# Moving one weight tile by 192 bytes and reordering two attention value products behind gate products

## The chip, the cores and the metric

The kernel runs on one core of one Trainium2 chip. The metric is the device time of one launch in microseconds (us), as the median of several runs. The layer has a batch of one, 512 positions and a model width of 1024, all in float32.

## What is computed

One decoder block with two mixers side by side, followed by a gated feed-forward. The core of the reference, shortened:

```python
h = rmsnorm(x, norm1_g)
a_b, a_c, a_x, q, kc, vc, ksl, vsl, kwn, vwn, g_nsa, g_merge = split(h @ w_in)
y_a = a_b * causal_dwconv(a_c * a_x, conv_a_w)
...                                    # q, k: norm and rotation; k_cmp, v_cmp: compressed keys and values
y_b = nsa(q, k_cmp, v_cmp, k_sel, vsl, k_win, vwn, sigmoid(g_nsa))
gm = sigmoid(g_merge)
x = x + (gm[:D] * (y_a @ w_a_out) + gm[D:] * (y_b @ w_b_out)) @ w_o
gu = rmsnorm(x, norm2_g) @ w_ffn_in
g = causal_dwconv(gu[:F], ffn_conv_w) + ffn_conv_b
x = x + (silu(g) * gu[F:]) @ w_ffn_out          # F = 2816
```

`nsa` has three branches per head: compressed keys, selected blocks and a sliding window. With 512 positions the selected blocks are all blocks, so the second and third branch are both plain causal attention with different keys and values.

## The kernel before

**Split products.** Every float32 operand is cut into a high and a low part in a faster format (`F32R` in the code). A product `w @ x` is then three products on PE: `wh@xh`, `wh@xl`, `wl@xh`. The helper `dense` issues first all `wh@xh` and `wh@xl` of an output tile (lines L437 and L438 of the profile), then all `wl@xh` (L440). The list that it returns holds only the first kind, in order: for a gate tile with eight input tiles these are 16 products, numbered 0 to 15.

**Order of work.** The program text lists the work stage by stage, but the order on each engine is made when the program is built. A planner goes through the instructions with its own estimates of their durations and starts on each engine the ready instruction that was written earliest. Each engine then runs its list strictly in order. `behind(later, earlier)` adds one rule for the planner: on that engine, `later` comes after `earlier`. It adds no wait to the running program.

**Attention.** `attend(pt_, g, qt)` handles one of two key groups `g` (four heads) for one block `qt` of 128 queries. Blocks are taken in the order 3, 2, 1, 0, and for each block `g` is 0 and then 1. For each branch `br` (1 first, then 0) PE makes the scores of each head into one of three banks of tag `s` (L665 and L666; L691 for block 0), DVE adds the mask and takes the maximum (L717, L718), ACT takes the exponential and thereby empties the bank (L719) and scales it (L725). The weights are then turned: a transpose on DVE (L652), four DMAs to memory and one back into a tile `tn` (`turn`). For each key tile `kt` ACT copies the high part (`ph`, L749), POOL subtracts it in place (L750), and PE adds two products to the block's accumulator `po`: the high product `ph` (L752) and the rest product (L759). They add to one accumulator and are issued in the order high, rest, high, rest. In branch 0 two products with the compressed values stand behind the first high product (L757); they need the tile `pc` that ACT writes at L743. At the end ACT copies half of the accumulator (`yt`, L761).

**Gate tiles.** `gate_tile(j, t)` makes one of 16 tiles of the merge gates. Its 24 products go to a bank of tag `d`. There are two such banks, and the conv tiles `pa`, the gate tiles `pg` and the mixer-A products `pma` take them in turn. In program order the stretch in question reads `pg2, pg3, pma2, pma3, pg4`, so `pg4` takes the bank that `pma2` had. That bank is emptied by DVE at L824. The planner fills PE with these products while attention waits for other engines. Two rules are written already: the first high product of block (g=0, qt=3) comes after product 6 of gate tile 0, and that of (g=0, qt=0) after product 10 of gate tile 13.

**Feed-forward.** Pairs of feed-forward tiles are computed as a Strassen product: seven products of half size instead of eight. `xf_h` and `xf_l` hold seven sums of input tiles as moving operands of 256 columns. `ff_forms` makes the weights' forms. `a22` is one quarter of the weights that is used as it is; its high part is the tile `th` (written by ACT at L173) and its low part the tile `tl`. The other forms are in `sh`, `sl` and in the ring `wh_s`, `wl_s`. The tiles lie one after another in each partition in the order of their first use; `gap_...` tiles hold nothing and only shift what follows. In the part that matters here the sizes in bytes of a partition are:

```
xf_h   4*7*256*4 = 28672
xf_l   4*7*256*4 = 28672
th     2 buffers of 2048
gap_w  48*4 = 192
tl     2 buffers of 2048
...    sf, sh, sl, p1: all multiples of 1024
```

Of the kernel before, what the change touches and what calls it, by code (L numbers as in the profile page):

```python
# [11 lines left out]
F32 = mybir.dt.float32  # L12
# [6 lines left out]
P = 128  # L19
# [66 lines left out]
def tile_block(ctx: ExitStack, tc: tile.TileContext, xT, pos, par, par2, w_tok, w_a3, w_gate, w_ao, w_bo, w_o,  # L86
               w_ff, w_dn, c_w1, out):
    nc = tc.nc
# [11 lines left out]
    def const(shape, name, dt=F32, pool=sb):  # L100
        return pool.tile(shape, dt, name=name, tag=name)
# [17 lines left out]
    def s_bank(name):  # L119
        return bank("s", name, 3)  # L120
# [3 lines left out]
    def t_bank(name, i=None):  # L124
        if i is None:
            i = len(n_t) % 2
            n_t.append(name)
        return bank(f"t{i}", name, 1)
# [55 lines left out]
    def ring_w(src, name):  # L184
        raw = raw_tile(name)
        nc.sync.dma_start(raw, src)
        h, l = ring(name)
        split(h, l, raw)
        return h, l
# [39 lines left out]
    def behind(later, earlier):  # L229

        tc.add_manual_dep(later.ins, earlier.ins.name,
                          mybir.DependencyInfo(mybir.DependencyClass.NoSync, mybir.DependencyReason.DATA),
                          reason="order")
# [206 lines left out]
            nc.tensor.matmul(acc, wl, xh, start=False, stop=last and i == len(units) - 1)  # L440
        return ops

    gate_ops, value_op = {}, {}

    def w_units(w, xh, xl, nk, k0=0, koff=0):
        wh, wl = w
# [6 lines left out]
    kHH, kL = kk[:, 0], kk[:, 1]  # L453
# [176 lines left out]
    def by_head(v, b):  # L630

        return v.rearrange("p (q a b i) -> p a b q i", q=QB, a=2, b=2)[:, :, b]

    def attend(pt_, g, qt):
        nk = (qt + 1) * P
        off = NC if qt < NT - 1 else 0
        q = qT[qt]
# [3 lines left out]
        def small(name, n, dt=F32):  # L641
            pool = pxg if name in ("mx1", "mx0", "sums1") else pb if name in ("sums0", "mcs") else pt_
            return pool.tile([P, HG, n], dt, name=f"{name}{tag}", tag=name, bufs=2)

        def e_tile(br, n):
            return pt_.tile([P, HG * S], F32, name=f"e{tag}{br}", tag="e", bufs=NE)[:, 0:n * HG * P].rearrange(
                "p (b k h i) -> p b k h i", b=QB, k=n, h=HG)

        def turn(e, n, e_name):

            v = e.rearrange("p b k h i -> p (b k h i)")
            nc.vector.transpose(v, v)  # L652
            w = n * P
            dst = pt_.tile([P, HG * S], F32R, name=f"tn_{e.name}", tag="tn", bufs=NTN)[:, 0:QB * w]
            d = dst.bitcast(F32)
            mid = dr.tile([QB, QB, SQ, w], F32, name=f"td_{e.name}", tag=f"td_{e.name}", bufs=1)
            for a in range(QB):
                nc.sync.dma_start(mid[a].rearrange("b j r -> j b r"),
                                  v[a * SQ:(a + 1) * SQ].rearrange("p (b r) -> p b r", b=QB))
            turned_dma[e_name] = nc.sync.dma_start(d.rearrange("p (a r) -> p a r", a=QB), mid.rearrange("a b j r -> (b j) a r"))  # L660
            return dst.rearrange("p (a k r) -> p a k r", a=QB, k=n)

        def scores(w, i, br, a, b):
            h = g * HG + i
            nc.tensor.matmul(w, q[:, h, :], kHH[:, 2 * br + g, a:b], start=True, stop=False)  # L665
            nc.tensor.matmul(w, q[:, h, :], kL[:, 2 * br + g, a:b], start=False, stop=True)  # L666

        def scale_of(sums, br):
            nc.vector.reciprocal(sums, sums)
            nc.gpsimd.tensor_mul(sums, sums, gates[:, :, br:br + 1])  # L670
# [10 lines left out]
        acc4 = acc.rearrange("p (a r) -> p a r", a=QB)  # L681
        if qt == 0:
# [4 lines left out]
            for i in range(HG):  # L687
                sc = s_bank(f"sc{tag}{i}")
                w = sc[:, 0:2 * (NC + P)].rearrange("p (b k) -> p b k", b=2)
# [15 lines left out]
        for br in (1, 0):  # L705
            if qt > 0:
                o = off if br == 0 else 0
                e = e_tile(br, qt + 1)
                mx = small(f"mx{br}", 1)
                sums = small(f"sums{br}", 1)  # L710
                for i in range(HG):
                    sc = s_bank(f"sc{tag}{i}{br}")
                    scores(sc[:, 0:o + nk], i, br, NC - o, NC + nk)
                    if o:
                        nc.vector.tensor_add(xc[:, i, :], sc[:, 0:NC], cm_add[:, qt, :])
                    dg = sc[:, o + nk - P:o + nk]
                    nc.vector.tensor_add(dg, dg, causal)  # L717
                    nc.vector.tensor_reduce(mx[:, i], sc[:, o:o + nk], axis=AX.X, op=ALU.max, negate=True)  # L718
                    nc.scalar.activation(e[:, :, :, i].rearrange("p b k i -> p k b i"),  # L719
                                         sc[:, o:o + nk].rearrange("p (k b i) -> p k b i", b=QB, i=SQ), AF.Exp,  # L720
                                         bias=mx[:, i], accum_out=sums[:, i])
                scale_of(sums, 1 + br)
                for i in range(HG):
                    v = e[:, :, :, i]
                    nc.scalar.activation(v, v, AF.Copy, scale=sums[:, i])  # L725
                turned = turn(e, qt + 1, (g, qt, br))
            if br == 0:
                mcs = small("mcs", 2)
                mc, sc_ = mcs[:, :, 0:1], mcs[:, :, 1:2]
                nc.vector.tensor_reduce(mc[:, :, 0], xc, axis=AX.X, op=ALU.max, negate=True)  # L730
                for i in range(HG):
                    nc.scalar.activation(xc[:, i], xc[:, i], AF.Exp, bias=mc[:, i], accum_out=sc_[:, i])
                scale_of(sc_, 0)
                nc.gpsimd.tensor_tensor(xc, xc, sc_.to_broadcast([P, HG, NC]), op=ALU.mult)
                xs = small("xs", 2 * NC, F32R)
                nc.scalar.activation(xs[:, :, 0:NC], xc, AF.Copy)
                nc.gpsimd.tensor_sub(xs[:, :, NC:], xc, xs[:, :, 0:NC].bitcast(F32))
                pt = t_bank(f"ptc{tag}", 0)
                for a in range(2):
                    nc.tensor.transpose(pt[:, a * P:(a + 1) * P],  # L740
                                        xs[:, 2 * a:2 * a + 2, :].rearrange("p h c -> p (h c)").bitcast(F32), ident)
                pc = pt_.tile([P, 2, P], F32R, name=f"pc{tag}", tag="pc", bufs=1)
                nc.scalar.activation(pc, pt[:, 0:2 * P].rearrange("p (a t) -> p a t", a=2), AF.Copy)  # L743
            k0 = br if qt == 0 else 0
            for kt in range(qt + 1):
                pl = turned[:, :, kt + k0]
                pt = pl.bitcast(F32)
                ph = pt_.tile([P, QB, P], F32R, name=f"ph{tag}{kt}{br}", tag="pth", bufs=NPT)
                nc.scalar.activation(ph, pt, AF.Copy)  # L749
                nc.gpsimd.tensor_sub(pl, pt, ph.bitcast(F32))  # L750
                w = v_t[:, kt, 2 * br + g, :]
                hi = nc.tensor.matmul(acc4, w, ph, start=kt == 0 and br == 1, stop=False)  # L752
                if kt == 0 and br == 1:
                    value_op[g, qt] = hi
                if kt == 0 and br == 0:
                    for b in range(2):
                        nc.tensor.matmul(by_head(acc, b), vc_t[:, b, g, :], pc.rearrange("p a (q i) -> p a q i", i=SQ),  # L757
                                         start=False, stop=False)
                nc.tensor.matmul(acc4, w, pl, start=False, stop=kt == qt and br == 0)  # L759
        tmp = pt_.tile([HD, 512], F32, name=f"yt{tag}", tag="yt", bufs=1)  # L760
        nc.scalar.activation(tmp, acc[HD:, :], AF.Copy)  # L761
        yo = pt_.tile([P, 2, P], F32, name=f"yo{tag}", tag="yo", bufs=1)
# [86 lines left out]
    for qt in QT_ORDER:  # L849
        for g in range(G):  # L850
            attend(pt_, g, qt)
# [18 lines left out]
    for i in range(4):  # L870
# [3 lines left out]
        w = ring_w(w_bo[i], f"bo{i}")  # L874
# [8 lines left out]
                                           op0=ALU.mult, op1=ALU.subtract)  # L883
    for w, step in (("ao1", (1, 3, 1)),):
        behind(raw_dma[w], turned_dma[step])
    for step, j, n in (((0, 3), 0, 6), ((0, 0), 13, 10),):
        behind(value_op[step], gate_ops[j][n])
    nc.scalar.activation(warm[:, 0:1], tb[KD - 1][:, 0:1], AF.Silu)
    in_ctx.close()

# [9 lines left out]
    xf_h = const([P, 4, 7, TH], "xf_h", F32R, px)  # L900
    xf_l = const([P, 4, 7, TH], "xf_l", F32R, px)
    pw = ctx.enter_context(tc.tile_pool(name="pw", bufs=1, side="left"))
    pw.tile([P, D // 2], F32R, name="th_", tag="th", bufs=2)
    const([P, 48], "gap_w", F32, pw)

    def x_forms(k, v):
        nc.vector.tensor_sub(v[:, T1:T3 + 1], v[:, 1:4:2], v[:, 0:2])
# [5 lines left out]
    for n, j in enumerate(O_ORDER):  # L913
        w = ring_w(w_o[j], f"o{j}")
# [275 lines left out]
```

## Time and profile before

| what | value |
|---|---|
| median of 3 runs | 696.2 us (695.93 to 697.58) |
| the profiled execution | 696.92 us, of which the span from the first to the last instruction is 695.1 us |
| PE busy | 689.2 us, 99% of the span, 4111 products |
| DVE, ACT, POOL busy | 74%, 63%, 36% of the span |
| granted TensorE clock | 1.000 |
| DMA | 124.87 MB, mean 180 GB/s |

The page gives the busy time of each engine. A busy PE may still be slower than it could be: what shows it is the distance from the start of one product to the start of the next. That distance is read from rows of the timeline, where the first column is the start in us and the second the duration. A mark in brackets at the end of a row is idle time of the engine just before it and what ended it.

### The profile page before, as it was taken

To read this page: it belongs to the slowest core of one execution; us is meant where nothing else is said; L and a number is where in the kernel's file an instruction comes from. 1 tells how busy PE (TensorE), PEld (TensorE's weight loads), DVE (VectorE), ACT (ScalarE), POOL (GpSimd) and SP (SyncE) were. 2 spreads that over 40 slices of the span, in tenths; PEclk is the share of its full clock that TensorE was granted. 3 is DMA by queue.
4 is the path that set the end of the run, shared out by engine and by line. 5 is a ranking of instruction groups with operands and counts; after the bars stand their busy time and mean duration, and the time that the engine had idled before them with its cause. 6 is when DMAs were issued, how large, how long until landed. Compare 5 with 4: busy or idle time off the path is not lost.

```text
span 695.1 us, 11268 instructions
## 1 busy us (share of the span) xinstructions
PE 689.2 (99%) x4111; PEld 614.5 (88%) x4111; DVE 511.7 (74%) x897; ACT 436.7 (63%) x776; POOL 248.7 (36%) x247
## 2 busy tenths in 40 slices
PE   9999999999999999999999999999999999999997
PEld 9999888887878888788889999999999999999986
DVE  6987886766566546475888999898787787877543
ACT  7635654878888866535776857665566655566530
POOL 4041443477788867462112212121122211112110
PEclk9999999999999999999999999999999999999999
DMA  8333686568666654563586977997877979775665
GB/s 268 113 98 122 170 194 145 132 240 237 222 222 228 195 169 124 193 229 118 130 198 160 219 192 167 245 218 180 215 173 180 210 172 227 174 175 112 132 137 152
DMA packets 57623, 124.87 MB, mean 180 GB/s; under 512 B 5344, under 2 KB 21088, under 8 KB 57568
## 3 DMA queue, kind: packets, MB, share of 16 engines
q1 hardware_dynamic: 35648, 79.39, 35.3%
q0 software_dynamic: 14848, 32.51, 27.4%
q10 hardware_dynamic: 7072, 12.26, 5.5%
q8 instruction: 32, 0.52, 0.3%
q14 instruction: 23, 0.19, 0.1%
HBM read 111.55 MB, written 12.58 MB: 179 GB/s over the span
## 4 chain that ended last, share of the span: by engine, by line
PE 95%; ACT 2%; DMA 1%; POOL 1%; DVE 1%; issue 0%; SPq 0%; ACTq 0%; POOLq 0%
PE p L438 10%; PE p L437 10%; PE p L440 10%; PE pdn L438 6%; PE pdn L437 6%; PE pdn L440 6%; PE pg L437 4%; PE pg L438 4%; PE pg L440 3%; PE pa L438 3%; PE pa L437 3%; PE pa L440 3%; PE po L438 2%; PE po L440 2%; PE po L437 2%; PE pj_s L269 2%
## 5 line engine op out<-in xcount | busy, mean ns | idle before, releaser
L437 PE MATMUL p<-xf_h,sh 128*128 128x256 f32 x336 | 80.6, 277 | 0.0
L438 PE MATMUL p<-xf_l,sh 128*128 128x256 f32 x336 | 80.5, 276 | 0.0
L175 POOL DMA_DIRECT2D wl_s<-in_w_ff_dram x22 | 19.6, 891 | 156.1 <-ACT wl_s L174 154.8
L438 PE MATMUL pdn<-al,wh_d 128*128 128x512 f32 (+1 forms) x176 | 68.5, 389 | 0.0
L437 PE MATMUL pdn<-ah,wh_d 128*128 128x512 f32 (+1 forms) x176 | 68.3, 389 | 0.0
L438 PEld LDWEIGHTS p<-xf_l,sh 128*128 128x128 f32 x336 | 63.1, 188 | 0.0
L437 PEld LDWEIGHTS p<-xf_h,sh 128*128 128x128 f32 x336 | 63.1, 188 | 0.0
L167 ACT ACTIVATE sh<-s 128x1024 fp32r<-128x1024 f32 x44 | 46.3, 1055 | 25.3 <-PE p L438 22.4
L168 DVE TENSOR_TENSOR sl<-s,sh 128x1024 fp32r<-128x1024 f32 x44 | 53.5, 1218 | 8.7 <-ACT sh L167 8.6
L173 ACT ACTIVATE wh_s<-wr_s 128x1024 fp32r<-128x1024 f32 x22 | 23.3, 1060 | 56.9 <-PE pdn L438 54.3
L750 POOL TENSOR_TENSOR tn_e<-tn_e,ph 128x512 fp32r<-128x512 f32 x40 | 51.2, 1294 | 16.2 <-ACT ph L749 16.0
L440 PE MATMUL p<-xf_h,sl 128*128 128x256 f32 x336 | 52.2, 277 | 0.0
L175 POOL DMA_DIRECT2D wl_d<-in_w_dn_dram x22 | 26.7, 1212 | 71.3 <-ACT wl_d L174 71.3
L437 PE MATMUL pg<-xg_h,wh_g 128*128 128x512 f32 x128 | 50.1, 392 | 0.0
L438 PE MATMUL pg<-xg_l,wh_g 128*128 128x512 f32 x128 | 50.1, 391 | 0.0
L440 PE MATMUL pdn<-ah,wl_d 128*128 128x512 f32 (+1 forms) x176 | 47.5, 388 | 0.0
L440 PEld LDWEIGHTS p<-xf_h,sl 128*128 128x128 f32 x336 | 44.7, 188 | 0.2
L1109 DVE TENSOR_TENSOR x<-x,pdn 128x512 f32<-128x512 f32 x47 | 32.0, 682 | 15.9 <-PE pdn L440 15.3
L150 POOL TENSOR_TENSOR wl_g<-wr_g,wh_g 128x1024 fp32r<-128x1024 f32 x16 | 38.5, 2405 | 10.4 <-ACT wh_g L148 9.7
L438 PE MATMUL p<-xf_l,wh_s 128*128 128x256 f32 x168 | 40.6, 277 | 0.0
L437 PE MATMUL p<-xf_h,wh_s 128*128 128x256 f32 x168 | 40.5, 277 | 0.0
L175 POOL DMA_DIRECT2D tl<-in_w_ff_dram x22 | 19.7, 894 | 57.3 <-ACT tl L174 49.7
(367 smaller groups left out, 2117.5 us busy)
## 6 DMA issues: line engine op xcount, KB each, us to landing
wr_s<-in_w_ff_dram SPq DMA_DIRECT2D x44, 512.0 KB, 5.0
wl_s<-in_w_ff_dram POOLq DMA_DIRECT2D x22, 512.0 KB, 7.8
wr_d<-in_w_dn_dram ACTq DMA_DIRECT2D x22, 512.0 KB, 8.3
wl_d<-in_w_dn_dram POOLq DMA_DIRECT2D x22, 512.0 KB, 9.0
wr_g<-in_w_gate_dram SPq DMA_DIRECT2D x16, 512.0 KB, 4.0
wr_a<-in_w_a_dram SPq DMA_DIRECT2D x12, 512.0 KB, 3.7
tl<-in_w_ff_dram POOLq DMA_DIRECT2D x22, 256.0 KB, 7.6
td_e<-e SPq DMA_DIRECT2D x16, 256.0 KB, 4.4
```

The lines of the kernel that those rows point to most:

```text
L150: e.tensor_sub(lo[:, 0:n], raw[:, 0:n], hi[:, 0:n].bitcast(F32))
L167: hi = nc.scalar.activation(h, v, AF.Copy)
L168: nc.vector.tensor_sub(l, v, h.bitcast(F32))
L173: nc.scalar.activation(h, raw, AF.Copy)
L175: nc.gpsimd.dma_start(l if dst is None else dst, src, accum_op=ALU.add)
L269: nc.tensor.matmul(acc, xg_h[:, k, ts_], wh, start=k == 0, stop=False)
L437: ops.append(nc.tensor.matmul(acc, wh, xh, start=first and i == 0, stop=False))
L438: ops.append(nc.tensor.matmul(acc, wh, xl, start=False, stop=False))
L440: nc.tensor.matmul(acc, wl, xh, start=False, stop=last and i == len(units) - 1)
L750: nc.gpsimd.tensor_sub(pl, pt, ph.bitcast(F32))
L1109: nc.vector.tensor_add(xj, xj, acc)
```

## The change

There are two edits. The empty tile `gap_w` of 192 bytes is allocated ahead of `th` instead of behind it. So both buffers of `th` lie 192 bytes higher, and every other tile stays where it is. And two rules for the planner are added to the two that exist: the first high product of block (g=1, qt=0) comes after product 13 of gate tile 14, and the rest product of block (g=1, qt=3), branch 0, key tile 2 comes after product 3 of gate tile 4. The products are recorded in dictionaries for this; `score_op` is recorded and not used.

```diff
-    gate_ops, value_op = {}, {}
+    gate_ops, value_op, rest_op, score_op = {}, {}, {}, {}
...
-                if kt == 0 and br == 1:
-                    value_op[g, qt] = hi
+                value_op[g, qt, br, kt] = hi
...
-                nc.tensor.matmul(acc4, w, pl, start=False, stop=kt == qt and br == 0)
+                rest_op[g, qt, br, kt] = nc.tensor.matmul(acc4, w, pl, start=False, stop=kt == qt and br == 0)
...
-    for step, j, n in (((0, 3), 0, 6), ((0, 0), 13, 10),):
-        behind(value_op[step], gate_ops[j][n])
+    for op, j, n in ((value_op[0,3,1,0], 0, 6),
+                     (value_op[0,0,1,0], 13, 10),
+                     (value_op[1,0,1,0], 14, 13),
+                     (rest_op[1,3,0,2], 4, 3)):
+        behind(op, gate_ops[j][n])
...
     pw = ctx.enter_context(tc.tile_pool(name="pw", bufs=1, side="left"))
+    const([P, 48], "gap_w", F32, pw)
     pw.tile([P, D // 2], F32R, name="th_", tag="th", bufs=2)
-    const([P, 48], "gap_w", F32, pw)
```

More of the change, by code (lines that the diff above doesn't have):

```diff
@@ L664, in scores @@
             h = g * HG + i
-            nc.tensor.matmul(w, q[:, h, :], kHH[:, 2 * br + g, a:b], start=True, stop=False)
+            score_op[g, qt, br, i] = nc.tensor.matmul(w, q[:, h, :], kHH[:, 2 * br + g, a:b], start=True, stop=False)
             nc.tensor.matmul(w, q[:, h, :], kL[:, 2 * br + g, a:b], start=False, stop=True)
```

## The prediction

> **What bounds the kernel now.** I read the page first, then the waits of PE, then the products grouped by shape, and last the timeline at the three places that the change touches. From the page, the busy times and the chain that ended last:
>
> ```profile
> PE 689.2 (99%) x4111; PEld 614.5 (88%) x4111; DVE 511.7 (74%) x897; ACT 436.7 (63%) x776; POOL 248.7 (36%) x247
> ...
> PE 95%; ACT 2%; DMA 1%; POOL 1%; DVE 1%; issue 0%; SPq 0%; ACTq 0%; POOLq 0%
> ```
>
> PE is the bound from end to end: 99% busy, and 95% of the chain that ended last. So the change can only pay by making PE's products follow each other faster, or by closing holes in PE's list. The waits of PE after the start-up are a single row:
>
> ```profile
> PE po L752 <- ACT ph L749: 1.1, 1, 1.1
> ```
>
> There is one hole of 1.1 us, in front of a value product. Smaller holes are below the limit of this view and must be read from the distances of starts in the timeline. The two edits touch separate stretches of PE's list, so I cost them apart.
>
> **Edit one: `th` 192 bytes higher.** The products of 256 columns, grouped by shape (busy time, mean ns of one):
>
> ```profile
> L438 PE MATMUL p<-xf_l,wh_s 128*128 128x256 f32 x168 | 40.6, 277 | 0.0
> L437 PE MATMUL p<-xf_h,wh_s 128*128 128x256 f32 x168 | 40.5, 277 | 0.0
> ...
> L438 PE MATMUL p<-xf_l,th 128*128 128x256 f32 x84 | 21.1, 282 | 0.0
> L437 PE MATMUL p<-xf_h,th 128*128 128x256 f32 x84 | 21.0, 281 | 0.0
> ...
> L440 PE MATMUL p<-xf_h,tl 128*128 128x256 f32 x84 | 13.1, 277 | 0.0
> ```
>
> The same shape takes 277 ns with every weight tile shown but `th`, where it takes 281 and 282. The products with `tl` read the same moving form of the input as those with `th` (T4), so the moving side is not the cause. The distance of starts says it more sharply. One block of eight `th` products, its four `tl` products and the block of eight `wh_s` products behind them:
>
> ```profile
> 388.53 0.28 PE L437 MATMUL p<-xf_h,th 128*128 128x256 f32 x1
> ...
> 389.49 0.62 PE L440 MATMUL p<-xf_h,tl 128*128 128x256 f32 x4
> 389.94 0.28 PE L437 MATMUL p<-xf_h,wh_s 128*128 128x256 f32 x1
> ...
> 390.85 0.62 PE L440 MATMUL p<-xf_h,wl_s 128*128 128x256 f32 x4
> ```
>
> Eight `th` products take 389.49 - 388.53 = 0.96 us, 120 ns each; eight `wh_s` products take 390.85 - 389.94 = 0.91 us, 114 ns each. What sets `th` apart is its place. From the sizes in the code, `th` begins 28672 + 28672 = 57344 bytes behind `xf_h`, which is 224 times 256 and also 7 times 8192: weights and moving operand lie at the same place within any power of two up to 8192. `tl` begins 192 bytes beyond such a place. After the edit `th` has the very offset that `tl` has now, so I expect the pace that the tiles at that offset have. By durations the saving is (282 - 277) + (281 - 277) = 9 ns for two products, by starts 6 ns for each. Over the 84 + 84 products (the eight of the first pair left out) that is 84 x 9 = 0.76 us or 168 x 6 = 1.01 us. I take 0.95 us, nearer to the starts, since starts are what adds up on PE. The ends are 0, if the place is not the cause, and 1.2 us (7 ns, one more for rounding). A loss is excluded by the `tl` row: nothing else moves, and the new offset is one that runs at 277 already. The ACT copies that write `th` and the DMAs do the same work.
>
> The Trainium skill speaks against this edit: "SBUF — State Buffer", section "Who interferes with whom", gives PE two SBUF read ports, one for the moving operand and one for the weight load, calls them independent, and says that only the port pair shared by DVE and GpSimd causes contention. By that rule the place of `th` could not matter and this edit would save nothing. The trace does not agree as it stands: 282 against 277 ns for the same shape.
>
> **Edit two, first rule: the first high product of block (1,0) behind product 13 of gate tile 14.** PE's list there:
>
> ```profile
> 280.08 0.39 PE L438 MATMUL pg<-xg_l,wh_g 128*128 128x512 f32 x1
> 281.54 0.50 PE L752 MATMUL po<-ph,v_t 128*128 128x512 f32 x1 [1.07 <-ACT ph L749]
> 281.88 0.40 PE L437 MATMUL pg<-xg_h,wh_g 128*128 128x512 f32 x1
> ...
> 283.49 0.39 PE L438 MATMUL pg<-xg_l,wh_g 128*128 128x512 f32 x1
> 283.71 0.39 PE L759 MATMUL po<-tn_e,v_t 128*128 128x512 f32 x1
> 283.94 0.39 PE L752 MATMUL po<-ph,v_t 128*128 128x512 f32 x1
> ...
> 284.62 0.40 PE L757 MATMUL po<-pc,vc_t 128*128 128x256 f32 x2
> 284.85 0.40 PE L759 MATMUL po<-tn_e,v_t 128*128 128x512 f32 x1
> 285.08 0.63 PE L440 MATMUL pg<-xg_h,wl_g 128*128 128x512 f32 x2
> ```
>
> The row at 281.54 is the product that is moved. The row at 280.08 is product 5 of gate tile 14, and the eight from 281.88 to 283.49 are 6 to 13; 14 and 15 stand between 283.94 and 284.62. Products of this shape normally start 0.227 us apart (283.49 to 283.94 is two of them). The hole is 281.54 - 280.08 - 0.23 = 1.23 us, and the product after it comes 0.34 instead of 0.23 us later, so the wait costs 1.34 us in all. With the rule the eight gate products run in the hole, from 280.31 to 282.12, and the high product starts at 282.12. They use the bank and the weights that products 0 to 5 use already, so nothing holds them. What is late next is read on ACT and POOL:
>
> ```profile
> 280.86 0.63 ACT L749 ACTIVATE ph<-tn_e 128x512 fp32r<-128x512 f32 x1 [5.10 <-DMA tn_e<-td_e]
> ...
> 282.35 0.61 ACT L749 ACTIVATE ph<-tn_e 128x512 fp32r<-128x512 f32 x1
> ...
> 283.60 0.39 ACT L743 ACTIVATE pc<-ptc 128x256 fp32r<-128x256 f32 x1
> ```
> ```profile
> 281.57 1.29 POOL L750 TENSOR_TENSOR tn_e<-tn_e,ph 128x512 fp32r<-128x512 f32 x1 [2.33 <-ACT ph L749]
> 283.04 1.29 POOL L750 TENSOR_TENSOR tn_e<-tn_e,ph 128x512 fp32r<-128x512 f32 x1 [0.18 <-ACT ph L749]
> ```
>
> These times hang on a DMA that lands at 280.86 and not on PE, so they stay. The high part is there at 281.49, well ahead of 282.12. But the first rest product needs POOL's 281.57 + 1.29 = 282.86. In the old list eight gate products hid that; now they stand ahead of the high product, and if the planner keeps the rest of its list, the rest product follows at once: it is due at 282.35 and starts at about 282.92. The high product of branch 0 then starts at 283.26, gate products 14 and 15 fill up to 283.94, the two L757 wait for `pc` (283.99) and start at 284.04, and the last rest product waits for POOL's 283.04 + 1.29 = 284.33. The low gate products (L440) start at 284.62 to 284.73 instead of 285.08. So of 1.34 us about 0.4 comes home; the rest turns into waits for POOL. The ends: 1.34 us, if the planner puts low gate products of L440 between the high and the rest product, and 0, if the DMA lands in such a way that POOL ends 0.4 us later. I take 0.4, because the planner's list changes least that way.
>
> **Edit two, second rule: the rest product of block (1,3), branch 0, key tile 2 behind product 3 of gate tile 4.**
>
> ```profile
> 191.50 0.48 PE L752 MATMUL po<-ph,v_t 128*128 128x512 f32 x1
> 191.95 0.50 PE L759 MATMUL po<-tn_e,v_t 128*128 128x512 f32 x1
> 192.29 0.39 PE L752 MATMUL po<-ph,v_t 128*128 128x512 f32 x1
> 192.52 0.43 PE L665 MATMUL sc<-kk,qT 128*128 128x416 f32 x1
> ...
> 193.19 0.50 PE L759 MATMUL po<-tn_e,v_t 128*128 128x512 f32 x1
> 193.53 0.39 PE L437 MATMUL pg<-xg_h,wh_g 128*128 128x512 f32 x1
> ...
> 194.61 0.40 PE L438 MATMUL pg<-xg_l,wh_g 128*128 128x512 f32 x1
> ```
>
> The row at 191.95 is the product that is moved; 193.53 and 194.61 are products 0 and 3 of gate tile 4. From 191.50 to 194.84, where the next one starts, PE issues twelve products: eight of 0.227 us and four scores of 0.189 us, 2.57 us of work in 3.34 us. So 0.77 us is lost here, mostly to waits for POOL's subtractions. With the rule the rest product, and the high and the rest product of key tile 3 behind it in the same accumulator, wait until four gate products are through. Those have a wait of their own:
>
> ```profile
> 191.21 0.98 DVE L718 TENSOR_REDUCE mx<-sc 128x1 f32<-128x384 f32 x2
> ...
> 192.22 0.67 DVE L824 SCALAR_TENSOR_TENSOR ma<-ma,pma 128x512 f32<-128x512 f32 x1
> ```
> ```profile
> 191.77 0.58 ACT L719 ACTIVATE e<-sc,mx 128x384 f32<-128x384 f32 x1 [0.73 <-DVE mx L718]
> 192.25 0.19 ACT L719 ACTIVATION_READ_ACCUMULATOR e<-sc,mx 128x1 f32 x1
> ```
>
> Gate tile 4 takes the bank that L824 empties, and that ends at 192.89. The next scores take a bank that ACT's exponential empties at 192.44. So after 191.73 PE has nothing it may do until 192.44. Then come two scores (to 192.82), the first gate product at 192.95, three more and the other two scores (to 194.24), and the three value products (to 194.92); with 0.1 us for each of two restarts the end is at about 195.05 instead of 194.84. I take a loss of 0.2 us. The ends: a loss of 0.57, if the planner puts all scores behind the gate products, so that PE idles until 192.95 (192.95 + 0.11 + 11 products of 2.35 us = 195.41); a gain of 0.77, if the new order lets DVE empty the bank ahead of its two L718 and no hole is left. Behind it, the reader of this accumulator has time: ACT's copy comes 3 us later.
>
> ```profile
> 198.16 0.60 ACT L761 ACTIVATE yt<-po 64x512 f32<-64x512 f32 x1
> ```
>
> **The sum.** -0.95 - 0.4 + 0.2 = -1.15 us. The profiled execution took 696.92 us (695.1 us of span and 1.8 us around it), so it becomes 695.8 us. It stands 0.7 us above the median of 696.2 us; against the median the forecast is 695.1 us. About 0.3%, 2.1 us, is what a measurement of this kernel can tell from no change, so this counts as no change.
>
> **The rivals.** The first is that all three holes close: -0.95 - 1.34 - 0.77 = -3.06 us, 693.1 us, faster. For it speaks that PE is the bound at all three places, so each ns saved is a ns of time; against it speak the POOL rows, which end at 282.86 and 284.33 whatever PE does, and the DVE row that holds gate tile 4's bank until 192.89. It needs a planner that fills both places with other products.
>
> The second is that edit one does not do what it says: the place does not matter, and `th` is slow for another reason. Then the sum is -0.4 + 0.2 = -0.2 us, 696.0 us. Against it stands that `th` is written by the same kind of ACT copy and read in the same loop as `wh_s`, which runs at 277 ns; place is the difference that is left.
>
> The third is the slower one: the planner draws all five lists anew, and a shift of PE near 192 us moves one of ACT's or DVE's steps of the next blocks behind another, so that a turned block lands later and its first value product waits as the one at 281.54 does. The place is each value product after 195 us, the price 1.34 us each. One such wait makes the sum +0.2 us, and from three on (+2.9 us, 699.1 us) it would be measurably slower. For it speaks that the hole at 280 us came about in this way; against it, that of the value products only that one shows a wait in the view of waits.
>
> **How the numbers follow.** Forecast (edit one pays, edit two nearly nothing): 0.62, with its own range 694.2 to 696.5 us. All holes close, in whole or for the larger part: 0.22, faster. The place does not matter: 0.10, no change. New waits: 0.06, slower. So faster 0.22, the same 0.72, slower 0.06. The range from 693.2 to 697.0 us begins at the first rival (693.1) and ends 1 us above the second (696.0), since the highest of the three runs shown is 1.4 us above their median; it leaves out the third rival and the outer edge of the first.
>
> **What would show it.** Edit one: the `th` rows at 277 ns and eight starts in 0.91 us; if they stay at 281 and 282, that step is wrong. First rule: no wait of L752 for ACT in the view of waits, the eight gate products ahead of L752, and L759 with a wait for POOL behind it; if L440 products stand between, the gain is larger. Second rule: a hole of about 0.7 us behind the L752 near 191.5 us, ended by ACT or DVE; if there is none, the step is wrong in my disfavour. The prediction as a whole fails if PE's list differs from the old one at other places than these, which a wait at another value product would show.

## The result and the profile after

The change makes the kernel slower, by 0.8%. Its median is 702.26 us (701.89 to 703.07) against 696.2 us (695.56 to 697.58) of the kernel before in the same session: ratio 1.0082, 95% interval 1.007 to 1.0094. The forecast was 695.1 us, range 693.2 to 697.0. The span of the profiled execution grows from 695.1 to 701.3 us.

From the page of the changed kernel, the line of the engines:

```profile
PE 695.3 (99%) x4111; PEld 620.2 (88%) x4111; DVE 512.2 (73%) x897; ACT 436.6 (62%) x776; POOL 248.2 (35%) x247
```

Its waits of PE (total us, times, longest):

```profile
PE wu L198 <- POOL ones L193: 1.1, 1, 1.1
PE sc L665 <- ACT e L719: 0.6, 1, 0.6
PE pj_s L269 <- DVE xg_h L295: 0.5, 1, 0.5
```

PE has the same 4111 products, its waits add up to 2.2 us as before, and it is busy 6.1 us longer (695.3 - 689.2). So the loss lies in the products themselves. The products grouped by shape (busy us, mean ns of one):

```profile
L437 PE MATMUL p<-xf_h,sh 128*128 128x256 f32 x336 | 82.9, 279 | 0.0
...
L438 PE MATMUL p<-xf_l,wh_s 128*128 128x256 f32 x168 | 41.7, 279 | 0.0
...
L437 PE MATMUL p<-xf_h,th 128*128 128x256 f32 x84 | 20.9, 280 | 0.0
L438 PE MATMUL p<-xf_l,th 128*128 128x256 f32 x84 | 20.9, 280 | 0.0
```

The forecast read this table for `th`, and `th` did what was hoped for, in part: 280 instead of 281 and 282. But every other tile went from 277 to 279, though no other tile was moved. Starts show it more sharply. The timeline of PE at a block of eight `th` products:

```profile
388.78 0.28 PE L437 MATMUL p<-xf_h,th 128*128 128x256 f32 x1
...
389.72 0.63 PE L440 MATMUL p<-xf_h,tl 128*128 128x256 f32 x4
390.19 0.28 PE L437 MATMUL p<-xf_h,wh_s 128*128 128x256 f32 x1
...
391.14 0.63 PE L440 MATMUL p<-xf_h,wl_s 128*128 128x256 f32 x4
```

Eight `th` products now take 0.94 us (389.72 - 388.78), 118 ns each, instead of 120. But eight `wh_s` products take 0.95 us (391.14 - 390.19), 118 to 119 ns each, where they took 0.91. Everything runs at 118, here and, from 373.7 us on, to the end.

I add up the distances from start to start of the 1852 products of 256 columns behind 358 us. Before, the 176 with `th` take 20.93 us and the 1676 others 191.46; after, 20.77 and 197.82. So `th` gains 0.15 us and the others lose 6.36 us. Put the other way: up to 371 us the same product of PE's list starts 0.24 us earlier than before, and at the end 6.15 us later. About 1.0 us of this arises between 373.7 and 405 us, and it begins ahead of the first block of eight `th` products in that stretch (379.24 us), right behind a product of 512 columns at 373.48 us; so no such block starts it.

The profile of the kernel before holds the reason, at a place that the prediction did not look at. Below, the rows at 437.01 and 437.95 are an `sh` block and its low products, and the others are the `th` block that comes 7 us later, behind products of 512 columns:

```profile
437.01 0.28 PE L437 MATMUL p<-xf_h,sh 128*128 128x256 f32 x1
...
437.95 0.63 PE L440 MATMUL p<-xf_h,sl 128*128 128x256 f32 x4
...
442.99 1.07 PE L440 MATMUL pdn<-ah,wl_d 128*128 128x512 f32 x4
443.90 0.28 PE L437 MATMUL p<-xf_h,th 128*128 128x256 f32 x1
...
444.85 0.62 PE L440 MATMUL p<-xf_h,tl 128*128 128x256 f32 x4
445.30 0.28 PE L437 MATMUL p<-xf_h,wh_s 128*128 128x256 f32 x1
...
446.21 0.50 PE L440 MATMUL p<-xf_h,wl_s 128*128 128x256 f32 x3
```

Eight `sh` products take 0.94 us (437.95 - 437.01) ahead of the `th` block, and eight `wh_s` products 0.91 us (446.21 - 445.30) behind it. So the kernel before knows both paces: 118 ns from 406.3 to 412.7, 418.2 to 421.7 and 424.1 to 444.9 us, and 113 to 114 ns elsewhere behind 374 us but for `th`. Each of the three slow stretches ends right behind `th` products. Ahead of 373 us, in the first pair, both kernels run mostly at 118 ns, and there four `th` products in a row at 360.84 us leave PE slow. From 444.85 us on PE is fast to the last few products, and every half pair there (the 84 products of one half of a feed-forward pair) begins with a `th` block behind products of 512 columns.

My theory after this: PE has two paces for these products, each holds itself, products of 512 columns can leave it in the slow one, and a `th` block at the moving operand's place (a start that is the same modulo 256 bytes) brings it back to the fast one. The edit took that away. The rivals: the reordering did it, or any irregular place does what `th` did. Below, "distance" is the number of bytes, modulo 256, by which a weight tile starts above the moving operand.

### The profile page after: what moved, and what is told of

Its sections match the earlier page's. It is cut to its first block, busy times and chain, and to the rows that moved or that the text cites. A ratio compares the mean times of both kernels' runs of the same rounds, so it can differ in the third digit from the quotient of the medians.

```text
span 701.3 us, 11266 instructions
## 1 busy us (share of the span) xinstructions
PE 695.3 (99%) x4111; PEld 620.2 (88%) x4111; DVE 512.2 (73%) x897; ACT 436.6 (62%) x776; POOL 248.2 (35%) x247
## 4 chain that ended last, share of the span: by engine, by line
PE 91%; DMA 3%; ACT 2%; issue 1%; POOL 1%; DVE 1%; SPq 0%; ACTq 0%; POOLq 0%; DVEq 0%
PE p L437 10%; PE p L440 10%; PE p L438 10%; PE pdn L437 6%; PE pdn L438 6%; PE pdn L440 6%; PE pg L437 4%; PE pg L438 3%; PE pg L440 3%; PE pa L438 3%; PE pa L437 3%; PE pa L440 3%; PE po L438 2%; PE po L437 2%; PE po L440 2%; PE pj_s L269 2%
## 5 line engine op out<-in xcount | busy, mean ns | idle before, releaser
L437 PE MATMUL p<-xf_h,sh 128*128 128x256 f32 x336 | 82.9, 279 | 0.0
L438 PE MATMUL p<-xf_l,sh 128*128 128x256 f32 x336 | 82.8, 279 | 0.0
```

Of the source, the lines that this page charges most:

```text
L437: ops.append(nc.tensor.matmul(acc, wh, xh, start=first and i == 0, stop=False))
L438: ops.append(nc.tensor.matmul(acc, wh, xl, start=False, stop=False))
```

## The experiments

Edits are given against the changed kernel. All times of the kernel before are those of the same session.

**Place alone.** The two new rules are left out, `th` stays where the change put it.

```diff
-                     (value_op[0,0,1,0], 13, 10),
-                     (value_op[1,0,1,0], 14, 13),
-                     (rest_op[1,3,0,2], 4, 3)):
+                     (value_op[0,0,1,0], 13, 10)):
```

> The changed place of th alone, with the two old rules; every engine's order is that of the kernel before. Theory A (pace): products of 256 columns have two paces that hold themselves, 113 and 118 ns from start to start, and a th block at the same place as the moving operand puts PE back to 113; without it the slow pace stays. Then 6.4 us are lost from 373 us on: about 702.6 us, and all weight tiles at 118 ns. Rival B (order): the slow pace came from the new order of value products, which changed what meets at the two L419 products at 373 us. Then this kernel is 0.9 us faster than before, about 695.3 us, with th at 113. Rival C (chance of the program): either pace can come out, without relation to th; the three rounds may then differ by 6 us among themselves.

Measured: 703.12 us against 696.95, ratio 1.0091 (1.0074 to 1.0107). By shape:

```profile
L438 PE MATMUL p<-xf_l,wh_s 128*128 128x256 f32 x168 | 41.7, 279 | 0.0
...
L437 PE MATMUL p<-xf_h,th 128*128 128x256 f32 x84 | 20.9, 280 | 0.0
```

The place alone makes the whole loss; the products of 256 columns take 218.6 us, as in the changed kernel. Its four runs lie between 702.72 and 703.69 us, so the pace is not drawn anew in every run.

**Rules alone.** `gap_w` goes back behind `th`, and all four rules stay.

```diff
+    pw.tile([P, D // 2], F32R, name="th_", tag="th", bufs=2)
     const([P, 48], "gap_w", F32, pw)
-    pw.tile([P, D // 2], F32R, name="th_", tag="th", bufs=2)
```

> The four rules with th at its old place; every engine's order is that of the changed kernel. Theory A: 113 ns for all tiles but th (120), and the gain of the rules alone: -0.8 us from the first, +0.3 us from the second, about 695.7 us. Rival B: about 702 us. Rival C: either.

Measured: 697.16 us against 696.95, ratio 1.0003 (0.9992 to 1.0013): no difference. `th` is back at 281 and 282 ns, the others at 276 and 277. The profiled execution has one wait that is not in the traces of before or after, and it comes from a weight DMA that landed late (PE's wait, then ACT's row):

```profile
PE pdn L437 <- ACT ah L167: 1.3, 1, 1.3
```
```profile
416.17 0.63 ACT L173 ACTIVATE th<-wr_s 128x512 fp32r<-128x512 f32 x1 [4.05 <-DMA wr_s<-in_w_ff_dram]
```

Such a late DMA costs about 1 us in one execution and nothing in another, and it is about as large as what the rules could bring.

**The low part at the old place.** If any tile at the moving operand's place brings the fast pace back, `tl` can take the part of `th`.

```diff
-    const([P, 48], "gap_w", F32, pw)
-    pw.tile([P, D // 2], F32R, name="th_", tag="th", bufs=2)
+    const([P, 48], "gap_w", F32, pw); pw.tile([P, D // 2], F32R, name="th_", tag="th", bufs=2)
+    const([P, 16], "gap_t", F32, pw); pw.tile([P, D // 2], F32R, name="tl_", tag="tl", bufs=2); const([P, 48], "gap_u", F32, pw)
```

> The changed kernel with th at its new place, and the low part tl moved on by 64 bytes so that it, and not th, lies at the same place modulo 256 as the moving operand; sf, sh and sl keep their place modulo 256. Order as in the changed kernel. Theory A says that any block at that place resets the pace, so tl's four products do it: tl at about 120 ns, th and all others at 113, about 695.5 us. If four products are too few or it must be the high part: 702 us, as changed.

Measured: 701.93 us, ratio 1.0071 (1.0056 to 1.0086). By shape:

```profile
L437 PE MATMUL p<-xf_h,wh_s 128*128 128x256 f32 x168 | 41.4, 279 | 0.0
...
L440 PE MATMUL p<-xf_h,tl 128*128 128x256 f32 x84 | 13.7, 283 | 0.0
```

Half an answer. `tl` now pays 283 ns, as any tile at that place seems to. In the fast stretch from 373.5 to 405.8 us PE is back at 113 ns behind every four `tl` products at 120: they do not end the fast pace. But where PE is slow, four of them do not bring the fast pace back, neither at 412 us among products of 256 columns nor from 421 us on behind products of 512 columns, where eight `th` products do in the kernel before.

**`th` 64 bytes higher.** `gap_w` is cut to 16 elements ahead of `th`, and 32 stand behind it.

> The changed kernel with th 64 instead of 192 bytes above its old place. Order as in the changed kernel. Theory A, if only the very same place modulo 256 resets the pace: 702 us as changed, all at 118 ns. If what matters is that th differs from the other weights, not that it agrees with the moving operand: th slow or not, the rest at 113, about 696 us.

Measured: 702.05 us, ratio 1.0072 (1.0057 to 1.0087). In its trace the `th` block runs at 113 to 114 ns where PE is fast, and behind it PE is fast at 378.6, 410.9 and 419 us. From 423 us on, where the `th` blocks stand behind products of 512 columns, it is not, and the tiles stay at 118 ns to the end (`th` itself at 119).

**Half of the `th` blocks.** If the `th` block at the old place resets the pace, a kernel with the old place in every second half pair must be fast in every second half pair. `th` gets one buffer at each of the two places.

```diff
-    const([P, 48], "gap_w", F32, pw)
-    pw.tile([P, D // 2], F32R, name="th_", tag="th", bufs=2)
+    pw.tile([P, D // 2], F32R, name="th0_", tag="th0", bufs=1); const([P, 48], "gap_w", F32, pw)
+    pw.tile([P, D // 2], F32R, name="th1_", tag="th1", bufs=1)
...
-        h = pw.tile([P, HALF_D], F32R, name=f"th{nm}", tag="th", bufs=2)
+        h = pw.tile([P, HALF_D], F32R, name=f"th{nm}", tag=f"th{n}", bufs=1)
```

> The changed kernel, but only the buffer of th that serves the first half of each feed-forward pair is back at its old place; that of the second half stays 192 bytes higher. Order as in the changed kernel. The pace theory (a th block at the moving operand's place ends the 118 ns pace, the 512-column products of the down projection bring it back): first halves at 113 ns behind their th block, second halves at 118 throughout, so about half of the 6.2 us comes back: 699 us. Rival (the place of th acts on the whole stage, or the pace is drawn once near 373 us and kept): 696 or 702 us, nothing between.

Measured: 701.34 us against 697.17, ratio 1.0062 (1.0045 to 1.0078). Two half pairs in a row, the first with `th` at the old place:

```profile
460.55 0.28 PE L437 MATMUL p<-xf_h,th 128*128 128x256 f32 x1
...
461.50 0.62 PE L440 MATMUL p<-xf_h,tl 128*128 128x256 f32 x4
461.95 0.28 PE L437 MATMUL p<-xf_h,wh_s 128*128 128x256 f32 x1
...
462.86 0.62 PE L440 MATMUL p<-xf_h,wl_s 128*128 128x256 f32 x4
...
475.57 0.28 PE L437 MATMUL p<-xf_h,th 128*128 128x256 f32 x1
...
476.52 0.63 PE L440 MATMUL p<-xf_h,tl 128*128 128x256 f32 x4
476.99 0.28 PE L437 MATMUL p<-xf_h,wh_s 128*128 128x256 f32 x1
...
477.93 0.63 PE L440 MATMUL p<-xf_h,wl_s 128*128 128x256 f32 x4
```

Behind the block at the old place eight `wh_s` products take 0.91 us, behind the block 192 bytes higher 0.94 us. It changes to and fro like this without exception from 461 to 659 us (fast from 461.50, slow from 476.52, fast from 491.89, slow from 506.92, and so on). The time is above the expected 699 us because PE was slow almost throughout from 374 to 461 us as well. That is in part a failure of the theory: the block of eight at 379.23 us has the old place, takes 0.96 us, and leaves PE as slow as it was, while the next one at the old place, at 398.69 us, does bring the fast pace.

**All tiles at the moving operand's place.** `gap_x`, ahead of `xf_h`, grows by 192 bytes and `gap_w` goes, so that `xf_h`, `xf_l` and every weight tile start at the same place modulo 256.

> The changed kernel with the moving forms xf_h and xf_l 192 bytes higher, and th, tl, sf, sh, sl where they are in the changed kernel, so that all weight tiles and the moving operands lie at the same place modulo 256. Order as in the changed kernel. If a product of 256 columns takes 120 ns whenever weights and moving operand share that place, as th did, all 1900 take 120: about 708 us, 6 ns x 1900 = 11 us over before. If th took 120 only because it differed from the other weight tiles, all alike gives 113 or 118: 694 to 702 us.

Measured: 706.45 us, ratio 1.0134 (1.0115 to 1.0154). By shape, products and then weight loads:

```profile
L438 PE MATMUL p<-xf_l,wh_s 128*128 128x256 f32 x168 | 42.4, 283 | 0.0
```
```profile
L437 PEld LDWEIGHTS p<-xf_h,wh_s 128*128 128x128 f32 x168 | 32.2, 192 | 0.1
```

All tiles run at 120 ns from start to start, and the 256-column products take 222.4 us. So the place does cost what edit one said: about 6 ns against the fast pace. The Trainium skill ("SBUF — State Buffer", section "Who interferes with whom") calls PE's two read ports, for the moving operand and for the weight load, independent. This experiment does not agree: against the changed kernel nothing but places differs, the tiles go from 118 to 120 ns, and the time from 1.0082 to 1.0134 times that of the kernel before.

**`th` 128 bytes higher.** `gap_w` is cut to 32 elements ahead of `th`, and 16 stand behind it.

> The changed kernel with th 128 instead of 192 bytes above its old place. Order as in the changed kernel. With 64 bytes th ran at 113 in the fast pace and its block ended the slow pace only where no 512-column product stood right before it. If 128 is like 64 or 192: about 702 us. If its block ends the slow pace behind 512-column products too, all tiles at 113: about 695 us, the best of all.

Measured: 702.91 us, ratio 1.0084 (1.0068 to 1.01). `th` runs at 119 ns, the rest at 118; the block at 378.78 us found PE fast and left it slow. So an odd place that costs a few ns is not enough to bring the fast pace back. That speaks against the second rival.

**The old place, the block issued late.** `th` is at the old place, and the product with `a22` is issued sixth of the seven instead of first, so that it no longer stands where the half pair begins.

```diff
-        product(b45[:, lo], "a22", T4)
         product(b1[:, lo], "a11", B11)
...
+        product(b45[:, lo], "a22", T4)
         product(b45[:, hi], 1, T1)
```

> The old place of th and the four rules, with the a22 product issued as the sixth of the seven in each half pair instead of the first; this changes the lists of all engines a little in the feed-forward stage. The pace theory: five of seven products run at 118 ns before the th block, only one at 113 behind it: 5/7 of the loss and th's 120 ns remain, about 701 us. Rival (it is enough that some weight tile lies at that place): 696 us.

Measured: 701.02 us, ratio 1.0058 (1.0042 to 1.0074). The timeline of PE around a `th` block:

```profile
464.76 0.28 PE L437 MATMUL p<-xf_h,sh 128*128 128x256 f32 x1
...
465.70 0.63 PE L440 MATMUL p<-xf_h,sl 128*128 128x256 f32 x4
466.18 0.28 PE L437 MATMUL p<-xf_h,th 128*128 128x256 f32 x1
...
467.13 0.62 PE L440 MATMUL p<-xf_h,tl 128*128 128x256 f32 x4
467.58 0.28 PE L437 MATMUL p<-xf_h,sh 128*128 128x256 f32 x1
...
468.49 0.62 PE L440 MATMUL p<-xf_h,sl 128*128 128x256 f32 x4
```

The same tile `sh` takes 0.94 us for eight products ahead of the block and 0.91 us behind it. From 466 us on PE falls back late in each cycle, always right behind products of 512 columns (596.8, 612.1, 627.4 us and so on), and the next `th` block brings it back (604.8, 620.1, 635.4). Both the reset and what undoes it are seen here. That the time met the expected 701 us is in part luck: PE was fast all through from 376 to 404 us and slow all through from 406 to 466 us, which the theory did not say. And the reset is not certain. Three whole `th` blocks of the same trace, at 407.90, 416.29 and 450.78 us, find PE slow and leave it slow:

```profile
450.78 0.28 PE L437 MATMUL p<-xf_h,th 128*128 128x256 f32 x1
...
451.74 0.64 PE L440 MATMUL p<-xf_h,tl 128*128 128x256 f32 x4
452.22 0.28 PE L437 MATMUL p<-xf_h,sh 128*128 128x256 f32 x1
...
453.16 0.63 PE L440 MATMUL p<-xf_h,sl 128*128 128x256 f32 x4
```

The `th` block takes 0.96 us (451.74 - 450.78), and the eight `sh` products behind it 0.94 us (453.16 - 452.22). These three and the one at 379.23 us of the kernel with half of the blocks stand behind other products of 256 columns. Every whole block that stands at the old place right behind products of 512 columns, in the kernel before and in this set of runs, brought the fast pace back.

**All weights at 64 bytes, and at 128.** The moving operand is shifted (`gap_x` 112 and 96 elements, `gap_w` 16 and 32), so that all weight tiles lie the same 64 or 128 bytes above its place and `th` is level with the others.

> The changed kernel, with all weight tiles (th, tl, sh, sl and their rings) 64 bytes above the moving operand's place modulo 256; th stays level with the others. Theory 'the distance decides' (64 bytes is a distance at which the slow pace does not hold, since th at 64 ended it three times in streams of 256 columns, at 378.6, 410.9 and 419 us): every group of the feed-forward at 113 to 114 ns from start to start, 212 us or less for the 256-column products of the stage, 694 to 696 us in all. Theory 'every place other than the moving operand's own is alike, and only products at that place free PE of the slow pace': 118 ns throughout, 218.6 us for the stage, 702 us in all. If weights level with the moving operand were slow for another reason than their distance, 120 ns and 706 us.

> The changed kernel, with all weight tiles 128 bytes above the moving operand's place modulo 256. Theory 'the distance decides': th alone at 128 ran at 119 ns and ended the fast pace, so all groups at 118 to 119 ns, 219 to 221 us for the stage's 256-column products, 702 to 704 us in all. Theory 'every place other than the moving operand's own is alike': 118 ns and 702 us. Fast throughout (113 ns, 695 us) would mean that what slowed th at 128 was the jump between two places and not the place.

Measured, against 697.59 us: 702.07 us (ratio 1.0061, 1.0045 to 1.0076) and 706.08 us (1.0123, 1.011 to 1.0136). By shape, first for 64 bytes and then for 128:

```profile
L438 PE MATMUL p<-xf_l,wh_s 128*128 128x256 f32 x168 | 41.6, 280 | 0.0
```
```profile
L438 PE MATMUL p<-xf_l,wh_s 128*128 128x256 f32 x168 | 42.4, 283 | 0.0
```

The theory that the distance decides falls in the first: at 64 bytes PE is fast from 373.0 to 405.0, 418.7 to 421.5 and 425.9 to 431.7 us and then slow to the end. The other theory's 702 us was met, but not its 118 ns throughout. So both paces hold themselves even where all weights lie alike, which is the clearest sign that the pace depends on what ran before and not on the place alone. The second came out like the one at distance zero (283 ns, 222.1 us for the 256-column products against 222.4). Neither theory gave that (702 to 704 us): for the steady pace, distances 0 and 128 are alike, and so may 64 and 192 be. This does not carry over to the reset, since `th` alone at 128 did not do what `th` alone at 0 does. In the three kernels with all weights alike, the weight tiles keep the place in memory that the changed kernel gives them, and only the moving operand moves; an effect of its own place is not ruled out, but `th` paid 120 and 119 ns at distances 0 and 128 with the moving operand unmoved.

**The first rule alone, old place.** The best that the change has to offer, if the second rule costs a little:

```diff
-                     (value_op[1,0,1,0], 14, 13),
-                     (rest_op[1,3,0,2], 4, 3)):
+                     (value_op[1,0,1,0], 14, 13)):
...
+    pw.tile([P, D // 2], F32R, name="th_", tag="th", bufs=2)
     const([P, 48], "gap_w", F32, pw)
-    pw.tile([P, D // 2], F32R, name="th_", tag="th", bufs=2)
```

> The kernel before with its layout, and the first of the two new rules alone (block (g=1, qt=0) behind product 13 of gate tile 14). If the rule closes the hole at 280 us for good: 0.4 to 0.8 us below before, ratio 0.9988 to 0.9994. If that hole is only as wide as the late transfer of one execution makes it: ratio 1.000 within its interval. Both new rules together gave 1.0003, so a loss by the second rule of 0.27 us is bought back here: 1.0000 at most.

Measured: 697.05 us (12 runs) against 697.59 (17 runs), ratio 0.999, interval 0.9981 to 1.0. This is the only version not above the kernel before, by about half a microsecond, and the interval reaches to no change. Its profiled execution was 1.0 us ahead of the one of before until 415 us and had lost that by 426 us, 0.7 us of it in one wait:

```profile
PE pdn L437 <- ACT ah L167: 0.7, 1, 0.7
```

ACT had waited 3.72 us for the same weight DMA just ahead of it. Whether the rule pays is left undecided between these two expectations.

## Why the prediction was wrong

**What bounds the kernel** was right: PE, by the pace of its products and by holes.

**Edit one is the step that failed.** Its sentence was: "A loss is excluded by the `tl` row: nothing else moves, and the new offset is one that runs at 277 already." The term of -0.95 us came out at +6.2 us (218.6 - 212.4 us for the 256-column products), and the place alone, without the rules, gives the whole loss. The cost of the place was read correctly: 120 ns at the moving operand's own place, in `th` before and in every tile where all lie there. Two things were taken for granted:

- That 277 ns belongs to the offset of `tl`. It belonged to the fast pace, in which PE was for most of the kernel before. The same tiles at the same offset ran at 118 ns in parts of that kernel and nearly throughout the changed one. So moving `th` gave it the slow pace: 0.15 us saved instead of 0.95.
- That an edit to 176 products can touch only those. The `th` block stands first in every half pair of 84 products, and what it leaves behind sets the pace of those that follow. The other 1676 products went from 114.2 to 118.0 ns on average, which is the 6.36 us.

The `tl` row of the view of groups could not tell this. The sign was in the timeline of the kernel before: products of one shape and one place at two paces in one execution, 0.94 us for eight at 437.01 and 0.91 us at 445.30.

**First rule**: right in its order and its waits. PE in the changed kernel, around the moved product (its L758 is L759 of the kernel before):

```profile
282.74 0.39 PE L752 MATMUL po<-ph,v_t 128*128 128x512 f32 x1
283.07 0.50 PE L758 MATMUL po<-tn_e,v_t 128*128 128x512 f32 x1
...
284.87 0.86 PE L440 MATMUL pg<-xg_h,wl_g 128*128 128x512 f32 x3
```

The list is the one forecast, the wait of L752 for ACT is gone, and the first rest product waits for POOL (283.07). The DMA's data reached ACT 0.15 us later here (281.01 against 280.86), so the low gate products, forecast for 284.62 to 284.73, were due at 284.77 to 284.88 and came at 284.87. Without the rule they would have started at 285.08 + 0.15 = 285.23: a gain of 0.36 us, forecast 0.4. That the size is so close is the agreement of one trace. In the drift between the traces it looks like 0.83 us, because PE came to this place 0.61 us late and the hole swallowed part of that. And the width of the hole differs between executions: with the place alone, without the rule, the data arrived at 280.30 and the row reads

```profile
280.98 0.50 PE L752 MATMUL po<-ph,v_t 128*128 128x512 f32 x1 [0.35 <-ACT ph L749]
```

PE's lag behind the kernel before shrinks here by 0.69 us without the rule, against 0.57 to 1.18 us in the traces that have it, so the traces do not give the rule's worth.

**Second rule**: right in its order and its hole; the size is not shown. PE in the changed kernel:

```profile
191.96 0.48 PE L752 MATMUL po<-ph,v_t 128*128 128x512 f32 x1
193.03 0.46 PE L665 MATMUL sc<-kk,qT 128*128 128x416 f32 x1 [0.59 <-ACT e L719]
...
193.52 0.47 PE L437 MATMUL pg<-xg_h,wh_g 128*128 128x512 f32 x1
...
194.89 0.39 PE L758 MATMUL po<-tn_e,v_t 128*128 128x512 f32 x1
```

A hole of 193.03 - 191.96 - 0.23 = 0.84 us ended by ACT's exponential, forecast about 0.7; over the stretch PE's lag grows from 0.46 to 0.73 us, a loss of 0.27, forecast 0.2. One trace does not settle that: over this stretch the lag changes by -0.30 to 0.35 us in the other traces with the rule, and by 0.14 and -0.56 us in the two without it (the place alone, the first rule alone).

**The rivals.** That all holes close did not happen. That the place does not matter is refuted by the experiment with all tiles at one place. The new waits in later blocks, the only rival on the slower side, did not come: the view of waits shows no wait of a value product. The loss came through the one edit for which the prediction had ruled a loss out. Among its rivals there was none in which the products at the old place do something for the others.

**What stays open**: what in PE holds a pace; why a `th` block at distance 0 resets it behind products of 512 columns, while one at 64, 128 or 192 bytes and four `tl` products at distance 0 do not; why four whole blocks at distance 0 behind products of 256 columns did not reset it; and what sets the pace at 374 us, where four kernels come out slow (the changed one, the place alone, `th` 64 bytes higher, half of the blocks), while two others without `th` at the old place come out fast (the low part, `th` 128 bytes higher).

## What to carry to other kernels

A duration of a group is not a property of its tile's place until the same place has been seen at one pace throughout: look for one shape at two paces within one execution, and ask what ran before each. Where one group of products is slower than its neighbours and stands regularly among them, test what it does to those behind it before it is sped up. And a hole that a DMA opens can have another width in the next execution (1.07 and 0.35 us of wait here, from data that came at 280.86 and 280.30 us): judge a rule that closes it by many runs, not by one trace.

## What the runs showed of the hardware

- Products of 256 columns, each with its own weights of 128 by 128, have two paces on PE at a granted clock of 1.000: 113 to 114 ns (276 to 277 ns a row) and 118 ns (279 to 280). Each holds itself over hundreds of products; nearly all changes come at products of 512 columns or `th` blocks. Products of 512 columns were followed by either pace. A whole feed-forward in the slow one costs 6.2 us here.
- With weights at the moving operand's own place modulo 256, or 128 bytes off it, in all tiles, the pace is a steady 120 ns (283 ns a row). Weight loads take 192 instead of 188 ns at distance zero and 189 at 128 bytes, so the longer load is not the whole of it.
- A block of eight products with weights at the moving operand's own place, 119 to 120 ns each, can put PE from 118 back to 113 ns. Behind products of 512 columns every whole one did; elsewhere four left PE slow. It is worth more than it costs here: 176 products some 5.5 ns slower than the fast pace, about 1 us, kept 1676 others some 4 ns faster than in the changed kernel.
